# Taking weights apart in one step of 1024 columns per engine, for those whose two low halves VectorE makes

## The chip, the cores and the metric

The kernel runs on one core of one Trainium2 chip. The core has five engines that each work through a queue of their own in order: TensorE (PE, matrix products; PEld are its weight loads), VectorE (DVE), ScalarE (ACT), GpSimd (POOL) and SyncE (SP), which here only issues DMAs. They wait for each other by semaphores. The metric is the device time of one execution in microseconds (us).

## What is computed

One layer of a hybrid model over 512 latent tokens and 256 context tokens, all in float32. The last part, in which most of this case plays, is a mixture of 16384 single-neuron experts:

```
px = split_in(modulate(x) @ w_in)            # projections of the tokens, 10240 columns
mix = merge(gates, hgrn(..), conv(..), att(..)) @ w_out
x = LN(alpha*x + gate*mix)
t = modulate(x)
s1, s2 = scores of 128 keys each, 8 heads    # q = t @ wq
expert, g = top 16 of the summed scores, softmax
act = gelu(u_tab[expert] . t)                # per token, head and k
peer = sum of g * act * v_tab[expert]
x = LN(alpha*x + gate2*peer)
```

The kernel computes the experts of 384 of the 512 tokens densely: all 128 blocks of 128 experts, `a = gelu(uT[i] . t)`, times a gate that is zero where an expert was not chosen, then `acc += a . v[i]`. The first 128 tokens are done by gathering the rows that they chose (256 rows per partition, from u and then from v).

## The kernel before

**Weights in two parts.** A float32 product is made of three faster ones: each operand x is taken apart into a rounded part `hi` and the rest `lo = x - hi`, and `mm3` (lines 140 to 144) adds lo.hi, hi.lo and hi.hi. A weight block is 128 partitions by 1024 columns (512 KB). `wload` (line 120) fetches one into a buffer `wraw` (three of these, SP issues the DMA on line 124 as soon as one is free), and takes it apart in two halves of 512 columns: ScalarE copies a half to `whi` (line 129), VectorE or GpSimd subtracts it into `wlo` (line 131). The argument `subs` names the engines of the two subtractions: (V, V) for 328 blocks, (V, G) or (G, G) for 80. `whi` and `wlo` have eight buffers of 512 columns each, so four blocks.

**Order.** PE, DVE, ACT and POOL run their instructions in the order in which the code is written. Only SP's DMAs are placed by a scheduler.

**Stages.** 590 to 790 us: the output products of the recurrence and the convolution; for each of eight j a merge-gate block (V, V) and a convolution block (V, G) are loaded. 790 to 1100: attention. 1200 to 1380: choice of the experts. 1380 to 1640: the first half of the dense products `uT`, beside the making of gates. From 1640 on the loop over the 128 expert blocks (the loop `for i in range(NT - LAST)` in the code).

**The loop.** Iteration i prepares block n = i + 1 and then multiplies block i. `weigh` makes VectorE multiply the activations by the gates (line 1601), and takes the product apart: ScalarE copies `ph` (line 137), VectorE subtracts `pl` (line 138). Then `wload` of v[n] follows: ScalarE copies `whi`, VectorE subtracts `wlo`. TensorE runs 18 products of 512 columns (`second`). Between them VectorE takes in one or two gathered rows (line 1488 for u, later 1496 for v, each 128x1024), which GpSimd fetches (line 1477). Up to iteration 69 (1640 to 1937 us) the activations were made before. From iteration 70 on (1937 to 2380 us) each iteration also loads u[n+1], right after `weigh`, runs 24 products of 384 columns (`first`) and takes in three or four rows; eight of these iterations have one VectorE step more (lines 1678 and 1681). Every eight iterations five DMAs fetch the next gates (`gr`, line 1589).

Of the kernel before, what the change touches and what calls it, by code (L numbers as in the profile page):

```python
# [9 lines left out]
F32 = mybir.dt.float32  # L10
F32R = mybir.dt.float32r
# [6 lines left out]
AF = mybir.ActivationFunctionType  # L18
# [4 lines left out]
T, TC, D, KT = 512, 256, 1024, 8  # L23
# [71 lines left out]
def body(tc, I, O):  # L95
    nc = tc.nc
    V, A, P, G = nc.vector, nc.scalar, nc.tensor, nc.gpsimd
# [8 lines left out]
    es = ExitStack()  # L106
    const = es.enter_context(tc.tile_pool(name="const", bufs=1))
    wes = ExitStack()
    wp = es.enter_context(tc.tile_pool(name="w", bufs=8))
    pms_ = ExitStack()  # L110
    pmm = pms_.enter_context(tc.tile_pool(name="pmm", bufs=3, space=PSUM))

# [7 lines left out]
    def wload(src, subs=(V, V), raw=None):  # L120

        raw = wp.tile([128, KT, 128], F32, name="wraw", bufs=3) if raw is None else raw
        if src is not None:
            nc.sync.dma_start(raw, src)
        his, los = [], []
        for i in range(2):
            r = raw[:, 4 * i:4 * i + 4, :]
            hi = wp.tile([128, 4, 128], F32R, name="whi")
            A.activation(hi, r, AF.Copy)  # L129
            lo = wp.tile([128, 4, 128], F32R, name="wlo")  # L130
            subs[i].tensor_sub(lo, r, hi.bitcast(F32))  # L131
            his.append(hi)
            los.append(lo)
        return his, los

    def split(hi, lo, src):
        A.activation(hi, src, AF.Copy)  # L137
# [124 lines left out]
    def fetch_next(n=3):  # L262

        if todo and len(ready) < n:
            w = todo.pop(0)
            src, subs = source(*w)
            if w[0] == 'ada':
                raw = wp.tile([128, KT, 128], F32, name="wraw", bufs=3)
                nc.sync.dma_start(raw, src)
                ready.append((w, raw))  # L270
                return
            ready.append((w, wload(None, subs, loaded.pop(0)) if loaded else wload(src, subs)))

    def feed(*w):
        fetch_next(1)
        tag, t_ = ready.pop(0)
        assert tag == w, (tag, w)
        return t_
# [35 lines left out]
    def ada_weights(q_):  # L314
        fetch_raw(7)
        return wload(None, (V, V) if not queue and not raws[1:] else (V, G), raws.pop(0))
# [711 lines left out]
    for g in range(4):  # L1028
        n = 8 * g
        if g == 3:  # L1030
            slot(n, (qb,), (qb,))
            m_ = chain([mgate(j) for j in range(KT)])
            for h in range(2):
                for i, nm in ((0, "kh"), (1, "kl")) if h == 0 else ((0, "vh"), (1, "vl")):
                    t_ = ap_.tile([128, T + TC] if h == 0 else [128, NS, 128], F32R, name=nm)
# [48 lines left out]
    for j in range(KT):  # L1084
        if j % 2 == 0:
            wout(j // 2)
        w = feed('att', j)
# [139 lines left out]
    parts1(0, tfs)  # L1227
    UV = {}
    UV['q', 0] = wload(I['wq'][0], (V, G))
    fetch_next(4)  # L1230
    turn_back(tfs)
# [216 lines left out]
    for b in range(1, NB):  # L1448
# [4 lines left out]
        sl = slice((b - 1) * 128, b * 128)  # L1453
# [341 lines left out]
```

## Time and profile before

| what | value |
|---|---|
| three runs, us | 2467.76 median, 2458.68 to 2470.45 |
| the profiled execution: its own time | 2469.7 |
| its span, first to last instruction | 2467.8 |
| mean granted TensorE clock (share of 2.4 GHz) | 0.986 |
| PE busy | 2356.6 us, 95% |
| DVE busy | 1937.8 us, 79% |
| ACT busy | 1044.3 us, 42% |
| POOL busy | 667.5 us, 27% |
| `wlo` on DVE, wraw blocks (680 of 512 columns) | 453.1 us busy, 186.1 us idle before them |
| `whi` on ACT, wraw blocks (784 of 512 columns) | 447.5 us busy |

The span is that of one profiled execution; 1.9 us of its own time lie around it. Busy shares are means over stages with different limits, and a busy PE is one with a matmul in flight, since matmuls overlap.

### The profile page before, as it was taken

What the parts mean: (1) busy time and instruction counts of PE and PEld (TensorE: products, weight loads), DVE (VectorE), ACT (ScalarE), POOL (GpSimd) and SP (SyncE); (2) the same over time, 40 slices, a digit from 0 to 9 for tenths busy, and PEclk for the clock granted to TensorE, in tenths of its full rate; (3) what the DMA queues carried; (4) which work ended last, traced back from release to release, by engine and by line L of the source; (5) the groups of instructions that cost most, each with busy time, mean ns of one, the idle gap of its engine ahead of it and who ended that gap; (6) DMA issues with size and microseconds to landing.
All of it is one profiled execution on the core that took longest, in us unless ns stands there. A gap on an engine that the chain in (4) does not pass through costs nothing.

```text
span 2467.8 us, 34756 instructions
## 1 busy us (share of the span) xinstructions
PE 2356.6 (95%) x12547; PEld 2028.7 (82%) x12547; DVE 1937.8 (79%) x3722; ACT 1044.3 (42%) x2298; POOL 667.5 (27%) x564
## 2 busy tenths in 40 slices
PE   7999999999988999999999999999999999999997
PEld 3888888887767777787899999987777889898886
DVE  7788888887665566564899789968878888889886
ACT  5544444434312444643457655533333333333333
POOL 6000000003122000031688401122323344444432
PEclk9999999999999999999999999999999999999999
DMA  6211111112364111132333368999999989999962
GB/s 243 69 60 61 61 60 60 52 65 72 134 212 158 43 35 35 52 111 103 105 112 103 121 241 308 330 321 317 335 368 348 350 317 344 324 336 320 331 223 96
DMA packets 156973, 452.66 MB, mean 183 GB/s; under 512 B 16256, under 2 KB 60672, under 8 KB 154624
## 3 DMA queue, kind: packets, MB, share of 16 engines
q1 hardware_dynamic: 106976, 278.33, 32.7%
q0 software_dynamic: 36864, 134.23, 15.3%
q10 hardware_dynamic: 12960, 37.87, 4.1%
q8 instruction: 99, 1.62, 0.3%
q14 instruction: 74, 0.61, 0.1%
HBM read 411.77 MB, written 37.03 MB: 182 GB/s over the span
## 4 chain that ended last, share of the span: by engine, by line
PE 57%; DVE 25%; DMA 6%; ACT 5%; issue 4%; POOL 2%; ACTq 0%; DVEq 0%; SPq 0%; POOLq 0%
PE mm L142 13%; PE mm L144 12%; PE mm L143 12%; DVE wlo L131 6%; DVE raw L1488 3%; DVE ttok L1496 3%; DMA wraw<-in_v_dram 3%; ACT whi L129 2%; PE sc L466 2%; PE pg L1538 2%; ACT ph L137 2%; DMA wraw<-in_uT_dram 2%; PE acc L142 1%; PE acc L143 1%; PE acc L144 1%
## 5 line engine op out<-in xcount | busy, mean ns | idle before, releaser
L131 DVE TENSOR_TENSOR wlo<-wraw,whi 128x512 fp32r<-128x512 f32 x680 | 453.1, 708 | 186.1 <-ACT whi L129 184.2
L142 PE MATMUL mm<-xh,wlo 128*128 128x512 f32 (+1 forms) x1456 | 559.7, 384 | 17.8 <-DVE wlo L131 5.5
L143 PE MATMUL mm<-xl,whi 128*128 128x512 f32 (+1 forms) x1456 | 540.3, 371 | 1.1 <-POOL xl L327 0.9
L144 PE MATMUL mm<-xh,whi 128*128 128x512 f32 (+1 forms) x1456 | 540.5, 371 | 0.0
L129 ACT ACTIVATE whi<-wraw 128x512 fp32r<-128x512 f32 x784 | 447.5, 621 | 121.3 <-DMA wraw<-in_w_in_dram 46.2
L142 PE MATMUL acc<-whi,pl 128*128 128x512 f32 x756 | 300.4, 397 | 23.9 <-DVE pl L138 18.8
L142 PEld LDWEIGHTS mm<-xh,wlo 128*128 128x128 f32 x1456 | 275.8, 189 | 53.1 <-DVE wlo L131 6.8
L144 PEld LDWEIGHTS mm<-xh,whi 128*128 128x128 f32 x1456 | 275.0, 189 | 37.2
L143 PEld LDWEIGHTS mm<-xl,whi 128*128 128x128 f32 x1456 | 275.8, 189 | 34.0 <-DVE xl L327 1.8
L143 PE MATMUL acc<-wlo,ph 128*128 128x512 f32 x756 | 301.5, 399 | 2.1 <-DVE wlo L131 0.9
L144 PE MATMUL acc<-whi,ph 128*128 128x512 f32 x756 | 298.6, 395 | 0.0
L1477 POOL DMA_INDIRECT raw<-in_u_dram,idx x128 | 147.4, 1151 | 472.1 <-DVE act L1488 413.5
L1477 POOL DMA_INDIRECT raw<-in_v_dram,idx x128 | 160.5, 1254 | 193.0 <-DVE ttok L1496 156.1
L142 PEld LDWEIGHTS acc<-whi,pl 128*128 128x128 f32 x756 | 143.8, 190 | 62.4 <-ACT whi L129 16.7
L137 ACT ACTIVATE ph<-a 128x384 fp32r<-128x384 f32 x94 | 49.4, 525 | 332.5 <-DVE a L1601 323.3
L561 DVE SCALAR_TENSOR_TENSOR u<-up,dw,u 128x512 f32<-128x512 f32 x240 | 179.6, 748 | 4.9
L131 POOL TENSOR_TENSOR wlo<-wraw,whi 128x512 fp32r<-128x512 f32 x104 | 149.2, 1457 | 123.0 <-ACT whi L129 116.6
L143 PEld LDWEIGHTS acc<-wlo,ph 128*128 128x128 f32 x756 | 143.7, 190 | 42.7 <-DVE wlo L131 13.4
L144 PEld LDWEIGHTS acc<-whi,ph 128*128 128x128 f32 x756 | 143.6, 190 | 28.5
L1496 DVE SCALAR_TENSOR_TENSOR ttok<-raw,act,ttok 128x1024 f32<-128x1024 f32 x127 | 162.9, 1283 | 3.1
L142 PE MATMUL pa<-xh,wlo 128*128 128x384 f32 x456 | 154.7, 339 | 6.4 <-DVE wlo L131 6.4
L144 PE MATMUL pa<-xh,whi 128*128 128x384 f32 x456 | 154.5, 339 | 0.0
(422 smaller groups left out, 4255.6 us busy)
## 6 DMA issues: line engine op xcount, KB each, us to landing
wraw<-in_uT_dram SPq DMA_DIRECT2D x128, 512.0 KB, 5.0
wraw<-in_v_dram SPq DMA_DIRECT2D x128, 512.0 KB, 6.2
wraw<-in_w_in_dram SPq DMA_DIRECT2D x96, 512.0 KB, 3.3
gd<-gs ACTq DMA_DIRECT2D x16, 1536.0 KB, 7.5
gr<-gd SPq DMA_DIRECT2D x60, 288.0 KB, 9.1
wraw<-in_w_adaT_dram SPq DMA_DIRECT2D x32, 512.0 KB, 4.4
wraw<-in_wq_dram SPq DMA_DIRECT2D x16, 512.0 KB, 3.3
ad<-a ACTq DMA_DIRECT2D x39, 192.0 KB, 4.2
```

The lines of the kernel that those rows point to most:

```text
L129: A.activation(hi, r, AF.Copy)
L131: subs[i].tensor_sub(lo, r, hi.bitcast(F32))
L137: A.activation(hi, src, AF.Copy)
L142: P.matmul(out, ll, rh, start=first, stop=False)
L143: P.matmul(out, lh, rl, start=False, stop=False)
L144: P.matmul(out, lh, rh, start=False, stop=last)
L466: P.matmul(x_.ps[:, b, :], x_.KM[:, b * 128:(b + 1) * 128], ap3(x_.QP, T + b * 128, [2 * w_, 64 // w_], [w_ - T, 2], [1, w_]), start=True, ...
L561: V.scalar_tensor_tensor(acc, up[:, i:i + T], dw[:, j, i:i + 1], acc, op0=ALU.mult, op1=ALU.add)
L1477: G.indirect_dma_start(out=r, out_offset=None, in_=I['u'] if n < NS_ else I['v'], in_offset=bass.IndirectOffsetOnAxis(ap=idx0[:, n % NS_:n ...
L1488: V.tensor_tensor_reduce(out=r, in0=r, in1=ttok, scale=1.0, scalar=0.0, op0=ALU.mult, op1=ALU.add, accum_out=act[:, s_:s_ + 1])
L1496: V.scalar_tensor_tensor(ysb, r, act[:, s_:s_ + 1], ysb, op0=ALU.mult, op1=ALU.add)
L1538: P.matmul(ps[:, i, :], o3[:, q_, :, i], o1[:, i, :], start=q_ == 0, stop=q_ == 1)
```

## The change

For (V, V) blocks ScalarE now copies all 1024 columns in one instruction and VectorE subtracts all 1024 in one. For the other blocks the two halves stay. `whi` and `wlo` become four buffers of 1024 columns, of the same size in all, and each comes free as a whole.

```
-    wp = es.enter_context(tc.tile_pool(name="w", bufs=8))
+    wp = es.enter_context(tc.tile_pool(name="w", bufs=4))
...
-        his, los = [], []
-        for i in range(2):
-            r = raw[:, 4 * i:4 * i + 4, :]
-            hi = wp.tile([128, 4, 128], F32R, name="whi")
-            A.activation(hi, r, AF.Copy)
-            lo = wp.tile([128, 4, 128], F32R, name="wlo")
-            subs[i].tensor_sub(lo, r, hi.bitcast(F32))
-            his.append(hi)
-            los.append(lo)
-        return his, los
+        halves = [slice(0, 4), slice(4, 8)]
+        hi = wp.tile([128, KT, 128], F32R, name="whi")
+        lo = wp.tile([128, KT, 128], F32R, name="wlo")
+        for sl, eng in ([(slice(0, 8), V)] if subs == (V, V) else zip(halves, subs)):
+            A.activation(hi[:, sl, :], raw[:, sl, :], AF.Copy)
+            eng.tensor_sub(lo[:, sl, :], raw[:, sl, :], hi[:, sl, :].bitcast(F32))
+        return [[t_[:, sl, :] for sl in halves] for t_ in (hi, lo)]
```

VectorE in the loop before 1937 us, one iteration before the change (gt and gr are activations and gates, ISA is the step that takes in a row):

```order
L1601 TENSOR_TENSOR gt<-gt,gr 128x384
L138 TENSOR_TENSOR pl<-gt,ph 128x384
L131 TENSOR_TENSOR wlo<-wraw,whi 128x512 x2
L1488 ISA raw,act<-raw,ttok 128x1024
L1488 ISA act 128x1
```

The same iteration after it (lines behind the edit are three lower):

```order
L1598 TENSOR_TENSOR gt<-gt,gr 128x384
L135 TENSOR_TENSOR pl<-gt,ph 128x384
L130 TENSOR_TENSOR wlo<-wraw,whi 128x1024
L1485 ISA raw,act<-raw,ttok 128x1024
L1485 ISA act 128x1
```

Two subtractions have become one, at the same place. ScalarE in the same iterations, before:

```order
L137 ACTIVATE ph<-gt 128x384
L129 ACTIVATE whi<-wraw 128x512 x2
L137 ACTIVATE ph<-gt 128x384
L129 ACTIVATE whi<-wraw 128x512 x2
L137 ACTIVATE ph<-gt 128x384
```

and after:

```order
L134 ACTIVATE ph<-gt 128x384
L129 ACTIVATE whi<-wraw 128x1024
L134 ACTIVATE ph<-gt 128x384
L129 ACTIVATE whi<-wraw 128x1024
L134 ACTIVATE ph<-gt 128x384
```

The copy stays behind `ph` of the same iteration, now as one instruction. Whatever waits for it waits for all 1024 columns. PE and POOL have the same instructions in the same order as before. SP's DMAs in the loop, before (`gr` are the gates, `wraw` the blocks of v):

```order
L124 DMA wraw<-in_v_dram 128x1024 x7
L1589 DMA gr<-gd 128x3x192 x3
L124 DMA wraw<-in_v_dram 128x1024
L1589 DMA gr<-gd 128x3x192
L1589 DMA gr<-gd 128x4x192
```

and after:

```order
L124 DMA wraw<-in_v_dram 128x1024 x7
L1586 DMA gr<-gd 128x3x192 x4
L124 DMA wraw<-in_v_dram 128x1024
L1586 DMA gr<-gd 128x4x192
L124 DMA wraw<-in_v_dram 128x1024 x7
```

One gate DMA more stands ahead of one v block, in four rounds of eight iterations; up to iteration 70 a few more DMAs trade places, and from there on SP's order is the same in both.

## Rows read from the trace of the kernel before

**Rows 1.** Stretches (span us, busy us and instructions, clock, DMA share, GB/s)
```profile
590.00:790.00 200.00, 177.59 (x751) 140.81 (x750) 122.95 (x183) 55.44 (x98) 50.90 (x29) 0.95 0.48 163
...
1640.00:1937.00 297.00, 284.30 (x1198) 221.47 (x1197) 241.24 (x423) 104.20 (x198) 86.20 (x79) 0.99 0.96 343
1937.00:2380.00 443.00, 426.70 (x2112) 383.99 (x2111) 382.46 (x505) 156.47 (x304) 197.39 (x156) 0.98 0.92 327
```

**Rows 2.** Chain that ended last, 1692 to 1712 (start, us, what)
```profile
1699.82 0.53 ACT ph L137
1700.35 0.53 ACT whi L129
...
1700.90 1.29 DVE wlo L131 x2
```

**Rows 3.** VectorE in order of time, 1694 to 1700 (start, us, instruction, idle before)
```profile
1695.05 0.55 DVE L1601 TENSOR_TENSOR gt<-gt,gr 128x384 f32<-128x384 f32 x1
1696.28 0.56 DVE L138 TENSOR_TENSOR pl<-gt,ph 128x384 fp32r<-128x384 f32 x1 [0.67 <-ACT ph L137]
1696.80 1.30 DVE L131 TENSOR_TENSOR wlo<-wraw,whi 128x512 fp32r<-128x512 f32 x2
1698.01 1.22 DVE L1488 CUSTOM_DVE_ANT_0 raw<-raw,ttok 128x1024 f32<-128x1024 f32 x1
...
1699.15 0.55 DVE L1601 TENSOR_TENSOR gt<-gt,gr 128x384 f32<-128x384 f32 x1
```

**Rows 4.** ScalarE in order of time, the same stretch
```profile
1696.15 1.14 ACT L129 ACTIVATE whi<-wraw 128x512 fp32r<-128x512 f32 x2
```

**Rows 5.** ScalarE groups by shape, whole span
```profile
L1072 ACT ACTIVATE xh<-wraw 128x1024 fp32r<-128x1024 f32 x4 | 4.2, 1048 | 1.9 <-DMA wraw<-in_w_out_dram 1.9
```

**Rows 6.** VectorE in order of time, 2218 to 2224
```profile
2220.74 1.22 DVE L1678 TENSOR_TENSOR gt<-gt 128x1024 f32<-128x1024 f32 x1
2221.88 1.29 DVE L131 TENSOR_TENSOR wlo<-wraw,whi 128x512 fp32r<-128x512 f32 x2
```

**Rows 7.** VectorE groups by shape, 1640 to 1937
```profile
L131 DVE TENSOR_TENSOR wlo<-wraw,whi 128x512 fp32r<-128x512 f32 x132 | 85.3, 688 | 8.9 <-ACT whi L129 8.9
```

**Rows 8.** VectorE groups by shape, 1937 to 2380
```profile
L131 DVE TENSOR_TENSOR wlo<-wraw,whi 128x512 fp32r<-128x512 f32 x202 | 130.2, 686 | 23.8 <-ACT whi L129 23.8
...
L1678 DVE TENSOR_TENSOR gt<-gt 128x1024 f32<-128x1024 f32 x4 | 4.9, 1217 | 0.0
L1681 DVE TENSOR_TENSOR gt<-gt 128x1024 f32<-128x1024 f32 x4 | 4.9, 1217 | 0.0
```

**Rows 9.** VectorE in order of time, 2155 to 2166
```profile
2157.28 0.56 DVE L138 TENSOR_TENSOR pl<-a,ph 128x384 fp32r<-128x384 f32 x1 [0.65 <-ACT ph L137]
2157.81 1.29 DVE L131 TENSOR_TENSOR wlo<-wraw,whi 128x512 fp32r<-128x512 f32 x2
```

**Rows 10.** Matmuls in order of time, 1699.5 to 1703
```profile
1699.49 0.39 PE L142 MATMUL acc<-whi,pl 128*128 128x512 f32 x1
...
1701.53 0.39 PE L142 MATMUL acc<-whi,pl 128*128 128x512 f32 x1
```

**Rows 11.** TensorE's weight loads' waits, 1640 to 1937 (total us, times, longest)
```profile
PEld acc L142 <- ACT whi L129: 16.7, 15, 2.1
PEld acc L143 <- DVE wlo L131: 13.2, 45, 0.5
```

**Rows 12.** Chain that ended last, 720 to 756
```profile
735.16 3.53 DMA wraw<-in_w_in_dram
738.77 0.64 ACT whi L129
739.43 0.70 DVE wlo L131
740.17 0.50 PE mm L142
```

**Rows 13.** VectorE's waits, 790 to 1100
```profile
DVE wlo L131 <- ACT whi L129: 27.3, 13, 4.3
```

## Prediction

> **What bounds the kernel now.** I read the table of stretches first. TensorE is busy nearly all the time everywhere, but the two long loop stretches (1640 to 1937 and 1937 to 2380 us) leave it 13 and 16 us short, and the merge-gate stretch (590 to 790 us) 22 us [rows 1]. A busy PE only says that a matmul was in flight, so next I asked for the chain of work that ended last. In the first loop stretch there is no matmul in it: it goes round from ScalarE's `ph` to its `whi`, to VectorE's `wlo` and on through VectorE to the next `ph` [rows 2]. VectorE in order of time says the same. Its cycle runs from one gate product to the next, 1695.05 to 1699.15, so 4.10 us; it has a single gap, 0.67 us, in which it waits for `ph`, and ScalarE can make `ph` only from the gate product that VectorE has just finished [rows 3]. TensorE needs about as long: nine matmuls take 1701.53 - 1699.49 = 2.04 us, so the 18 of an iteration 4.08 [rows 10]. A second row taken in makes VectorE's cycle longer by what one row holds it, 1698.01 to 1699.15, 1.14 us [rows 3], and TensorE's not at all; accordingly it is TensorE that waits for the weights, 45 times for `wlo` and 15 times for `whi` [rows 11]. So a wait that is added to VectorE's cycle there is added to the time, for TensorE has no more than 0.02 us of need beyond the cycle, and nothing else on VectorE's path can run meanwhile.
>
> **What the change does to one iteration.** Now ScalarE starts the two `whi` copies at 1696.15 [rows 4], and VectorE starts on `wlo` at 1696.80 [rows 3]. The chain shows how the two hang together: the first copy ends at 1700.35 + 0.53 = 1700.88, and the subtraction of that half begins 0.02 us later, while the second half is still being copied [rows 2]. That overlap is what goes. A copy of 1024 columns from a `wraw` buffer is in the trace: 1048 ns [rows 5]. Begun at 1696.15, behind the same `ph`, it ends at 1697.20, and with 0.02 us for the signal VectorE starts at 1697.22, so 0.42 us later. What VectorE gets back: the two halves hold it from 1696.80 to the next start at 1698.01, 1.21 us [rows 3]; a float32 product of 1024 columns holds it from 2220.74 to 2221.88, 1.14 us [rows 6]. That is 0.07 us. Net +0.35 us per iteration. Behind the waiting subtraction stand the taking in of a row and the next gate product, so `ph`, `whi` and TensorE's next weights all come that much later.
>
> The Trainium skill, Perfetto Trace Analysis, section Optimizing Scalar/DVE Operations, puts the fixed cost of a VectorE instruction on SBUF at about 60 ns and says that grouping pays if the engine is saturated; the 0.07 us above agrees. By that rule alone each block would be about 0.06 us cheaper and the kernel faster (the third rival). The same section ends by saying that breaking up instructions lets work complete sooner where they cause bubbles on other engines, which is this cycle's case.
>
> **The sum, by stretches.**
> 1. 1640 to 1937 us: 132 halves, so 66 blocks [rows 7], each in the cycle above: 66 x 0.35 = +23.1 us. Blocks whose DMA lands late cost the same, since VectorE then waits for the copy anyhow.
> 2. 1937 to 2380 us: 202 halves, 101 blocks [rows 8]. Fifty are u blocks, loaded right behind `pl`; there VectorE goes from `pl` to `wlo` without a gap, as it does in the first stretch [rows 3, 9], so these too get +0.35. In eight of them a step of 1024 columns stands between, 4 + 4 in number and 1.22 us long [rows 8], which covers the copy: -0.07. The 51 v blocks are subtracted after three or four rows have been taken in, long after their copy: -0.07. Sum 42 x 0.35 - 59 x 0.07 = 14.7 - 4.1 = +10.6. VectorE's cycle is the path here also: its 382 us busy and its waits of 24 us for late copies [rows 1, 8] and about 0.65 us for each of 50 `ph` [rows 9] make 439 of 443 us.
> 3. 590 to 790 us: eight merge-gate blocks come one after another out of a loop that runs over a DMA. The block lands, `whi` starts at 738.77, `wlo` at 739.43, and TensorE's first product at 740.17, as soon as the first half is subtracted [rows 12]. With whole blocks the copy ends at 739.82, the subtraction of 1.22 us (the 1024 columns of [rows 6]) at 741.06, and TensorE starts 0.9 us later than now. If TensorE came late by itself, only the raw buffer's later return would count, 0.35. I take 0.8, near the upper end, as the row shows TensorE waiting: 8 x 0.8 = +6.4.
> 4. 790 to 1100 us: 13 waits of VectorE for `whi` [rows 13], each longer by 0.35, half of them on the path by my choice: +2.3, between 0 and 4.6.
> 5. Elsewhere TensorE sets the pace with its weights fetched two or three blocks ahead: 0, at most +4.
> 6. Paid back: VectorE waits 8.9 and 23.8 us for copies in the two loop stretches [rows 7, 8], almost all of it for blocks of v and u still on their way, with the DMA engines 96% and 92% busy [rows 1]. With a longer iteration a block has more time to land, about 0.9 us in the first stretch (its buffer is asked for two and a half iterations ahead), 0.4 in the second, and the engines less to carry per us. Bounds: nothing and all of it, -33. I take -9. Against this, SP sends one gate DMA of 288 KB more ahead of a block in four rounds; at 343 GB/s [rows 1] that is 0.84 us each, 0 to +3.4, taken as 0 since a block has some slack in most rounds.
>
> The buffers that come free as a whole cost nothing that I can see: a block takes the place of the one four earlier, and in the loop ScalarE's copy stands behind `ph`, which has to wait for products that come after that block's. Should this cover fail, the copy waits half a block's products, up to 2.04 us [rows 10]. Blocks with GpSimd keep their halves: 0.
>
> Sum 23.1 + 10.6 + 6.4 + 2.3 - 9 = +33.4 us against the profiled execution's own 2469.7, so 2503.1. That execution is 1.9 us above the median of the three runs; against the median, 2467.8, the forecast is 2501 us.
>
> **Rivals.**
> - *The DMA waits give it all back.* The 32.7 us of waits vanish as the loop slows: 23.1 + 10.6 + 6.4 - 32.7 = +7.4, so 2475 us. For it: DMA engines nearly full. Against it: a burst of five gate DMAs lands on top of the blocks every eight iterations whatever the pace, and one iteration's 0.3 us more can't take up waits of several us each. Chance 0.08.
> - *TensorE's clock falls.* The merge-gate stretch, with TensorE 11% idle, was granted a clock of 0.95, the loop 0.99 and 0.98 [rows 1]. With 23 us more idle time the first loop stretch would be at (12.7 + 23.1) / 320 = 11% as well. There it costs nothing, since VectorE's cycle is by then the longer; in the second, 4% on 427 us of matmuls would be +17: 2518 us, or a little more with no payback. Chance 0.08.
> - *Faster: fewer instructions, and the wait isn't there.* If VectorE found the copy ready, it would save 0.07 us on each of 66 + 101 blocks, -11.7, and the time would be 2456 us. This is decided at one point: the whole copy must end before `pl` does, at 1696.84, so it would have to start 0.39 us sooner than 1696.15; but ScalarE is at `ph` until then [rows 2, 4], and its order is fixed. Chance 0.04.
>
> **How the numbers follow.** The forecast has a chance of 0.8. Its own range: with all of the payback that seems likely (-20) and 3 us less elsewhere 2487; with no payback and the upper ends of terms 4 to 6 2520. To hold 8 in 10 with the case of full payback half in it, I give 2482 to 2520. A measurement of this kernel can tell about 0.5% from no change, so "same" is 2455 to 2480: it holds the rival of full payback, and a sliver of the forecast: 0.08. Faster than that is a good half of the third rival, 0.03. Slower: 0.89.
>
> **What the next profile would show.** In the first loop stretch VectorE's cycle at 4.45 us instead of 4.10, with a new gap of about 0.4 us ahead of each `wlo` ended by `whi`, one `whi` of 1.05 us and one `wlo` of 1.22 us; TensorE's waits for `wlo` up by some 20 us; the stretch longer by about 20 us. In the second the gap only ahead of the u blocks. In the merge-gate stretch TensorE's start on a block 2.3 us after `whi` starts. I am wrong if that gap is missing, if the cycle stays at 4.10 with the gap there (then something I took for the path had slack), or if the waits for late blocks shrink by as much as the gaps add.

## The result, and the profile after

The changed kernel takes 2494.86 us (median, 2493.89 to 2500.97), the one before 2463.73 us in runs beside it: a ratio of 1.0129, interval 1.0101 to 1.0158. It is slower by 31 us; the forecast was 2501. The profiled execution took 2500.97 us, 31.3 more than that of before; both lie some 6 us above their medians. Line numbers behind the edit are 3 lower now (`ph` and `pl` L134 and L135, the gate product L1598); `whi` stays L129 and `wlo` is L130.

The stretches after, in the columns of [rows 1]:
```profile
590.00:790.00 200.00, 174.19 (x737) 137.77 (x736) 122.63 (x167) 54.28 (x86) 46.80 (x30) 0.96 0.49 161
1640.00:1937.00 297.00, 276.88 (x1119) 206.09 (x1118) 222.86 (x334) 91.62 (x125) 80.41 (x73) 0.99 0.92 321
1937.00:2380.00 443.00, 423.69 (x2079) 375.06 (x2078) 371.49 (x411) 145.86 (x202) 211.45 (x155) 0.99 0.92 329
```
The clock is no lower than it was. Inside the same 297 us VectorE is 18 us and TensorE 7 us less busy than in [rows 1], and TensorE gets through 1119 matmuls instead of 1198. Both engines lost time, so something holds them up in turn. VectorE and ScalarE in order of time, 1701 to 1707 us (start, us, instruction, idle time before it and what ended it), answer to [rows 3, 4]:
```profile
1701.93 0.55 DVE L1598 TENSOR_TENSOR gt<-gt,gr 128x384 f32<-128x384 f32 x1
...
1703.03 1.04 ACT L129 ACTIVATE whi<-wraw 128x1024 fp32r<-128x1024 f32 x1
1703.16 0.56 DVE L135 TENSOR_TENSOR pl<-gt,ph 128x384 fp32r<-128x384 f32 x1 [0.67 <-ACT ph L134]
1704.11 1.23 DVE L130 TENSOR_TENSOR wlo<-wraw,whi 128x1024 fp32r<-128x1024 f32 x1 [0.39 <-ACT whi L129]
1705.25 1.22 DVE L1485 CUSTOM_DVE_ANT_0 raw<-raw,ttok 128x1024 f32<-128x1024 f32 x1
...
1706.39 0.55 DVE L1598 TENSOR_TENSOR gt<-gt,gr 128x384 f32<-128x384 f32 x1
```
The cycle is 1706.39 - 1701.93 = 4.46 us (4.10 before). The 0.67 us for `ph` is as it was; new is 0.39 us for `whi` ahead of `wlo`. The copy starts 0.13 us before `pl` as before, but `wlo` now has to wait for 1.04 us of it instead of 0.53. The single subtraction holds VectorE from 1704.11 to 1705.25, 1.14 us, as the sum had it.

VectorE's group for `wlo`, first the first loop stretch, then the second [rows 7, 8], and last the waits of TensorE's weight loads in the first [rows 11]:
```profile
L130 DVE TENSOR_TENSOR wlo<-wraw,whi 128x1024 fp32r<-128x1024 f32 x62 | 76.0, 1225 | 35.0 <-ACT whi L129 35.0
```
```profile
L130 DVE TENSOR_TENSOR wlo<-wraw,whi 128x1024 fp32r<-128x1024 f32 x100 | 122.2, 1222 | 33.9 <-ACT whi L129 30.8 <-PE pa L141 2.3 <-PE pa L139 0.8
```
```profile
PEld acc L140 <- DVE wlo L130: 38.2, 59, 1.1
PEld acc L139 <- ACT whi L129: 11.0, 14, 1.8
```
In the first stretch VectorE's idle time ahead of `wlo` goes from 8.9 to 35.0 us, and TensorE's wait for `wlo` from 13.2 to 38.2. In the second VectorE's goes only from 23.8 to 33.9.

Both traces hold the same 12,547 matmuls in the same order, so the delay can be read matmul by matmul. By stretches of the kernel before, the changed one loses: 100 to 590 +1.3; 590 to 790 +3.6; 790 to 1100 +0.6; 1100 to 1380 -0.3; 1380 to 1640 +1.3; 1640 to 1937 +21.4; 1937 to 2380 +0.6; from there to the end +2.9; 31.4 in all.

In the merge-gate stretch a block looks like this (ScalarE, VectorE and TensorE, 698 to 703 us; compare [rows 12]):
```profile
698.89 1.06 ACT L129 ACTIVATE whi<-wraw 128x1024 fp32r<-128x1024 f32 x1 [5.75 <-DMA wraw<-in_w_in_dram]
699.99 1.23 DVE L130 TENSOR_TENSOR wlo<-wraw,whi 128x1024 fp32r<-128x1024 f32 x1 [3.05 <-ACT whi L129]
701.26 0.50 PE L139 MATMUL mm<-xh,wlo 128*128 128x512 f32 x1 [2.00 <-DVE wlo L130]
702.10 0.63 PE L139 MATMUL mm<-xh,wlo 128*128 128x512 f32 x1
```
From the copy's start to TensorE's start it is 701.26 - 698.89 = 2.37 us (1.40 in [rows 12]; 2.3 was forecast). The last row shows a second price: 0.84 us after the wait of 2.00 us matmuls hold TensorE 0.63 us instead of 0.39. The granted clock from 702 to 705 us is 0.51 of 2.4 GHz, the 1.2 GHz level.

### The profile page after: what moved, and what is told of

It reads as the page before. It is cut to its first block, busy times and chain, and to the rows that moved or that the text cites. A ratio compares the mean times of both kernels' runs of the same rounds, so it can differ in the third digit from the quotient of the medians.

```text
span 2499.2 us, 33937 instructions
## 1 busy us (share of the span) xinstructions
PE 2364.8 (95%) x12547; PEld 2021.9 (81%) x12547; DVE 1917.3 (77%) x3394; ACT 1012.3 (41%) x1970; POOL 687.3 (28%) x564
## 4 chain that ended last, share of the span: by engine, by line
PE 31%; DVE 24%; ACT 7%; DMA 6%; issue 4%; POOL 1%; ACTq 0%; SPq 0%; POOLq 0%; DVEq 0%
PE mm L139 6%; PE mm L141 6%; PE mm L140 6%; DVE wlo L130 6%; DVE raw L1485 4%; ACT whi L129 4%; DVE ttok L1493 3%; DMA wraw<-in_v_dram 2%; DMA wraw<-in_uT_dram 2%; PE pg L1535 2%; ACT ph L134 2%; DVE eb L1339 1%; PE pa L139 1%; DVE a L1598 1%; PE pa L141 1%
## 5 line engine op out<-in xcount | busy, mean ns | idle before, releaser
L130 DVE TENSOR_TENSOR wlo<-wraw,whi 128x1024 fp32r<-128x1024 f32 (+1 forms) x353 | 428.4, 1217 | 247.9 <-ACT whi L129 230.6
L129 ACT ACTIVATE whi<-wraw 128x1024 fp32r<-128x1024 f32 (+1 forms) x457 | 417.3, 929 | 107.0 <-DMA wraw<-in_w_in_dram 39.7
L140 PE MATMUL acc<-wlo,ph 128*128 128x512 f32 x756 | 304.2, 402 | 16.5 <-DVE wlo L130 11.5
L1474 POOL DMA_INDIRECT raw<-in_u_dram,idx x128 | 152.5, 1192 | 490.8 <-DVE act L1485 431.4
L1474 POOL DMA_INDIRECT raw<-in_v_dram,idx x128 | 174.4, 1362 | 178.5 <-DVE ttok L1493 141.4
L134 ACT ACTIVATE ph<-a 128x384 fp32r<-128x384 f32 x94 | 49.4, 525 | 395.2 <-DVE a L1598 377.0
L130 POOL TENSOR_TENSOR wlo<-wraw,whi 128x512 fp32r<-128x512 f32 x104 | 147.1, 1436 | 130.3 <-ACT whi L129 126.2
```

The source lines that it names most:

```text
L129: A.activation(hi[:, sl, :], raw[:, sl, :], AF.Copy)
L130: eng.tensor_sub(lo[:, sl, :], raw[:, sl, :], hi[:, sl, :].bitcast(F32))
L140: P.matmul(out, lh, rl, start=False, stop=False)
L1474: G.indirect_dma_start(out=r, out_offset=None, in_=I['u'] if n < NS_ else I['v'], in_offset=bass.IndirectOffsetOnAxis(ap=idx0[:, n % NS_:n ...
```

## The experiments

The theory: the price is VectorE's wait for the end of a 1024-column copy, paid where VectorE comes to `wlo` right behind `pl` (or right behind a landing block) and its cycle sets the pace. The rivals: the four buffers, the mere length of either instruction, or a pace set elsewhere. Times are medians; each is set against the kernel before in runs beside it (2464.0 to 2466.1 us).

**Four whole buffers, but halves in both engines.**
```diff
-        for sl, eng in ([(slice(0, 8), V)] if subs == (V, V) else zip(halves, subs)):
+        for sl, eng in zip(halves, subs):
```


> The changed kernel with its four whole buffers, but every block is again copied in two steps of 512 columns by ScalarE and subtracted in two steps of 512 by VectorE. Theory (the price is VectorE's wait for a copy of 1024 columns): the time of the kernel before, 2464 us within 8, and in the first loop's stretch VectorE's cycle is back at 4.10 us from 4.46. Rival (a block's buffers now come free only as a whole, so transfers or copies start later): about the changed kernel's 2495, and the cycle stays near 4.46.


Measured: 2460.66 us, ratio 0.9983 (0.9967 to 0.9999). In the first loop stretch VectorE's group for `wlo` is that of [rows 7] again:
```profile
L130 DVE TENSOR_TENSOR wlo<-wraw,whi 128x512 fp32r<-128x512 f32 x135 | 87.4, 688 | 6.2 <-ACT whi L129 6.2
```
The median cycle of iterations 3 to 65 is 4.16 us again, as before the change (4.51 in the changed kernel). So the buffers are not the loss, and that rival is out. SP's DMAs, however, stand here in the order of the kernel before and not of the changed one, so this run alone does not tell the whole steps from the new order. The trace of the changed kernel does: there the copy starts 0.13 us ahead of `pl` as before, so its block has landed, and the new gap lies behind the copy's start. The whole steps are the loss. The buffers alone gain some 4.7 us (0.2 to 8 by the interval), which neither theory expected. By the matmuls the stretch from 590 to 790 is 5.5 us shorter. The clock there differs (665 to 785 us, columns as in [rows 1]), first before, then this kernel:
```profile
665.00:785.00 120.00, 100.70 (x410) 78.79 (x409) 70.81 (x102) 25.07 (x46) 32.55 (x16) 0.93 0.62 208
```
```profile
665.00:785.00 120.00, 101.32 (x433) 78.67 (x432) 74.13 (x107) 25.55 (x47) 29.19 (x16) 0.97 0.65 211
```
More on this in the last section.

**VectorE in one step, ScalarE in two.**
```diff
-        for sl, eng in ([(slice(0, 8), V)] if subs == (V, V) else zip(halves, subs)):
+        for sl, eng in zip(halves, subs):
             A.activation(hi[:, sl, :], raw[:, sl, :], AF.Copy)
-            eng.tensor_sub(lo[:, sl, :], raw[:, sl, :], hi[:, sl, :].bitcast(F32))
+            if subs != (V, V):
+                eng.tensor_sub(lo[:, sl, :], raw[:, sl, :], hi[:, sl, :].bitcast(F32))
+        if subs == (V, V):
+            V.tensor_sub(lo, raw, hi.bitcast(F32))
```


> The changed kernel with ScalarE's copy in two steps of 512, VectorE's subtraction still in one of 1024. Theory (what counts is when the whole of `whi` is there): the second half's copy ends 1.16 us after the first one's start, against 1.05 for the one copy, so VectorE starts about 0.1 later than in the changed kernel: cycle 4.55 to 4.57 against 4.46, time 2495 + 66 x 0.1 + 42 x 0.1 = about 2505. Rival (the length of ScalarE's single copy is itself the harm, for example because the product's copy `ph` queues behind it): ScalarE's copies are as before, so the time goes back to about 2465.


Measured: 2510.16 us, ratio 1.0176 (1.0155 to 1.0197). In order of time, 1708 to 1714 us:
```profile
1708.76 0.55 DVE L1601 TENSOR_TENSOR gt<-gt,gr 128x384 f32<-128x384 f32 x1
...
1709.86 1.14 ACT L129 ACTIVATE whi<-wraw 128x512 fp32r<-128x512 f32 x2
1709.98 0.56 DVE L138 TENSOR_TENSOR pl<-gt,ph 128x384 fp32r<-128x384 f32 x1 [0.67 <-ACT ph L137]
1711.02 1.23 DVE L133 TENSOR_TENSOR wlo<-wraw,whi 128x1024 fp32r<-128x1024 f32 x1 [0.48 <-ACT whi L129]
...
1713.31 0.56 DVE L1601 TENSOR_TENSOR gt<-gt,gr 128x384 f32<-128x384 f32 x1
```
The two copies end at 1711.00, 0.09 later than one would, the gap is 0.48 and the cycle 4.55. What counts is when the last column of `whi` is there, and the length of ScalarE's instruction is not itself the harm. Against the changed kernel the first loop stretch costs 4 us more and the stretches up to 1100 us 6, where a copy's end counts as well; of the two loops the first was expected to cost 7, and the second, for which 4 were expected, costs nothing.

**ScalarE in one step, VectorE in two.**
```diff
-        for sl, eng in ([(slice(0, 8), V)] if subs == (V, V) else zip(halves, subs)):
-            A.activation(hi[:, sl, :], raw[:, sl, :], AF.Copy)
+        if subs == (V, V):
+            A.activation(hi, raw, AF.Copy)
+        for sl, eng in zip(halves, subs):
+            if subs != (V, V):
+                A.activation(hi[:, sl, :], raw[:, sl, :], AF.Copy)
             eng.tensor_sub(lo[:, sl, :], raw[:, sl, :], hi[:, sl, :].bitcast(F32))
```


> ScalarE's copy in one step of 1024 columns, VectorE's subtraction in two of 512, four whole buffers. Theory (VectorE waits for the end of the whole copy): the gap of 0.39 us ahead of `wlo` stays and the 0.07 us that one subtraction saves is gone, so the cycle is 4.53 us and the time 2495 + 66 x 0.07 + 42 x 0.07 = about 2502. Rival (VectorE's instruction of 1024 columns is the harm): back near 2465.


Measured: 2500.76 us, ratio 1.0147 (1.0117 to 1.0177). VectorE in order of time, 1707 to 1713 us:
```profile
1707.88 0.55 DVE L1601 TENSOR_TENSOR gt<-gt,gr 128x384 f32<-128x384 f32 x1
...
1710.06 1.29 DVE L133 TENSOR_TENSOR wlo<-wraw,whi 128x512 fp32r<-128x512 f32 x2 [0.39 <-ACT whi L129]
...
1712.41 0.56 DVE L1601 TENSOR_TENSOR gt<-gt,gr 128x384 f32<-128x384 f32 x1
```
With VectorE's old two instructions the gap is there all the same, and the cycle is 1712.41 - 1707.88 = 4.53 us, as expected: gap 0.39, saving of 0.07 gone. VectorE's long instruction is not the harm.

**The `v` block fetched ahead of the weighing, in the first loop.**
```diff
+            if ('v', n) not in UV:
+                fetch(('v', n))
```


> The changed kernel, but in the first loop (iterations up to 69) the `v` block is fetched and taken apart ahead of the gathered rows' weighing instead of behind it; nothing is computed otherwise. Theory (the price is the wait for a copy that starts too late): ScalarE's copy now has other work of VectorE beside it or the wait moves; if the copy is done by the time VectorE comes to `wlo`, its cycle is 4.10 - 0.07 = 4.03 us and the time 2495 - 66 x 0.43 = about 2467; if VectorE comes to `wlo` first, the wait grows and the time stays above 2490. Rival (a step of 1024 columns costs VectorE or the DMA more than two of 512, wherever it stands): the cycle stays near 4.46 and the time near 2495 even where no gap stands ahead of `wlo`.


Measured: 2471.75 us, ratio 1.0024 (1.0012 to 1.0036). ScalarE and VectorE, 1847 to 1852 us:
```profile
1847.94 0.55 DVE L1598 TENSOR_TENSOR a<-a,gr 128x384 f32<-128x384 f32 x1
...
1849.09 1.05 ACT L129 ACTIVATE whi<-wraw 128x1024 fp32r<-128x1024 f32 x1
...
1850.83 1.22 DVE L130 TENSOR_TENSOR wlo<-wraw,whi 128x1024 fp32r<-128x1024 f32 x1
...
1851.97 0.55 DVE L1598 TENSOR_TENSOR a<-a,gr 128x384 f32<-128x384 f32 x1
```
`wlo` now comes behind a row's step, 0.69 us after its copy has ended; no gap, and a cycle of 4.03 us, with the same steps of 1024 columns. By the matmuls the stretch is back at the time of before (-0.8 us, against +21.4). It gains nothing beyond that; VectorE's idle time ahead of `wlo` is 19.5 us there, against 8.9 in [rows 7], and ScalarE's copies wait 21.6 us for blocks that land late, against 8.3 before:
```profile
L130 DVE TENSOR_TENSOR wlo<-wraw,whi 128x1024 fp32r<-128x1024 f32 x67 | 81.8, 1222 | 19.5 <-ACT whi L129 14.6 <-issue 4.8
```
The whole step costs nothing where its copy has ended. The time is 5 us above the 2467 expected.

**Whole steps in one place at a time**, all with four whole buffers. First the first loop's `v` blocks alone:
```diff
-        for sl, eng in ([(slice(0, 8), V)] if subs == (V, V) else zip(halves, subs)):
+        for sl, eng in ([(slice(0, 8), V)] if whole else zip(halves, subs)):
...
-        UV[item] = wload(src, SUBS[kind])
+        UV[item] = wload(src, SUBS[kind], whole=kind == 'v' and i < NU)
```


> Whole steps only for the `v` blocks of the first 71 iterations, halves in all other blocks (the two merges, the `u` blocks, the second loop's `v` blocks); four whole buffers. Theory: the first loop's stretch carries 66 x 0.36 = 23.8 less the DMA waits paid back, 21 us in the changed kernel's trace, so the time is 2464 + 21 = 2485, and the stretch from 1640 is as long as in the changed kernel. Rival (the time is lost by the steps elsewhere, the stretch only shows it): under 2475.


Measured: 2474.73 us, ratio 1.0037 (1.0023 to 1.0051). That lies under the bound set for the rival, but the mechanism is the theory's: in the trace the stretch loses 18.3 us, the median cycle is 4.51 us instead of 4.16 (iterations 3 to 65, two-row ones among them), and no other stretch loses more than 0.8. The expectation had started from before; from four buffers with halves, 2460.7, it is +14 by the times (the profiled execution was 5 us slower than the median).

The second loop's `v` blocks alone (`whole=kind == 'v' and i >= NU`):

> Whole steps only for the `v` blocks of the second loop (iterations 71 and later), where rows are weighed between the copy's start and `wlo` and no gap stood ahead of it; halves elsewhere; four whole buffers. Theory: no wait is added there and each such block saves VectorE 0.07 us, at most 51 x 0.07 = 3.6: 2460 us, or 2464 where it is not on the path. Rival (a whole step costs something besides the wait): above 2470.


Measured: 2460.81 us, ratio 0.9982 (0.9968 to 0.9996): no different from halves. VectorE's idle time ahead of the 50 whole ones from 1937 to 2380 us is small:
```profile
L130 DVE TENSOR_TENSOR wlo<-wraw,whi 128x1024 fp32r<-128x1024 f32 x50 | 61.0, 1220 | 2.4 <-ACT whi L129 2.4
```
So the blocks that I had called covered are covered; the 0.07 us that each should save does not show in the time.

All blocks but those of `u` and `v` (`whole=False` where these are loaded, else by `subs == (V, V)`):

> Four whole buffers; whole steps only outside the `u`, `v` blocks of the two loops and of the products behind the merges, that is in the merges and the products up to 1100 us; halves in every `u` and `v` block. Theory (the forecast's terms 3 and 2, now against the kernel with four whole buffers and halves, 2461, whose product that follows each gate's block of `wlo` started 1.2 us after TensorE's last): the changed kernel's trace against that one has +1.6 from 100 to 590, +9.0 from 590 to 790 and +2.0 from 790 to 1100, so the time is 2461 + 12.6 = 2473. Rival (what that trace lost from 590 to 790 is TensorE's granted clock of that one run, not the whole step): 2461 + 4 = 2465.


Measured: 2473.43 us, ratio 1.0035 (1.002 to 1.0049). TensorE's waits for `wlo` from 590 to 800 us, with four buffers and halves, then here:
```profile
PE mm L139 <- DVE wlo L130: 16.5, 9, 2.0
```
```profile
PE mm L139 <- DVE wlo L130: 21.7, 14, 2.1
```
+5.2 us of waits, and the clock from 665 to 785 us is at 0.94, as in the changed kernel, instead of 0.97. By the matmuls 590 to 790 is 6.7 us longer than with halves, and 1.5 and 2.0 us are lost in the stretches around it. The theory's 12.6 is met, 12.0 by the differences to before. An estimate of the clock's share from these two traces: from 640 to 800 us 31 matmuls follow each other at 0.42 us here and 17 with halves; 14 more at 0.19 us each are 2.7 of the 6.7 us, so the longer part is the wait.

The `u` blocks alone (`whole=kind == 'u'`):

> Four whole buffers; whole steps only for the `u` blocks (50 of them in the second loop, the others from 1380 to 1640), halves elsewhere. Theory (VectorE's cycle sets the second loop's pace too): 42 blocks with no rows ahead lose 0.26 each as in the changed kernel's trace, 10.9, and 1.3 from 1380 to 1640: 2461 + 12 = 2473. Rival (the second loop is bound by the DMA, so the wait for the copy takes the place of a wait for the transfer; the changed kernel's trace lost only 0.6 there): 2461 + 2 = 2463.


Measured: 2467.50 us, ratio 1.0008 (0.9998 to 1.0019), between the two. VectorE's groups for `wlo` from 1937 to 2380 us:
```profile
L130 DVE TENSOR_TENSOR wlo<-wraw,whi 128x512 fp32r<-128x512 f32 x98 | 63.1, 685 | 0.7 <-ACT whi L129 0.6
L130 DVE TENSOR_TENSOR wlo<-wraw,whi 128x1024 fp32r<-128x1024 f32 x50 | 61.2, 1224 | 31.6 <-ACT whi L129 31.2 <-PE pa L141 0.4
```
All of the wait stands ahead of the `u` blocks: 42 x 0.39 = 16.4 us is the copy, the other 15 are late transfers, which were 20.3 in the kernel with halves. So a part of the wait for the copy takes the place of one for the transfer: the commonest cycle is 8.37 us instead of 8.01, but the time grows by 6.1 us in place of 12 (against four buffers with halves, each by its difference to before).

Set against four buffers with halves, each by its difference to before in its own runs, the places add up: 14.1 (first loop) + 1.5 (second loop's `v`) + 12.0 (merges) + 6.1 (`u`) - 4.7 (buffers) = +29, where the whole change has +31. Each term is uncertain by some 4 us, as the intervals show.

**The other end of the same rule: fill VectorE's gap.** If VectorE's cycle sets the pace, then taking out its other wait, the 0.67 us for `ph`, must make the kernel before faster. One row's step moves to between `ph` and `pl` (and the second loop keeps one row back for it):
```diff
-        split(ph[i2][0], ph[i2][1], a_)
+        A.activation(ph[i2][0], a_, AF.Copy)
+        if todo:
+            todo.pop(0)()
+        V.tensor_sub(ph[i2][1], a_, ph[i2][0].bitcast(F32))
...
```


> The kernel before, with one gathered row's step moved, in each weighing, from behind the product's subtraction `pl` to between its copy `ph` (ScalarE) and `pl` (VectorE). In the first loop VectorE waits 0.67 us there for `ph`; the moved step has 0.6 to 0.7 us of work. Theory (VectorE's cycle of 4.10 us, waits included, sets the first loop's pace): the cycle falls towards 3.45, until TensorE or the DMA bounds it; TensorE has 276.9 us of work in that stretch of 297, so 10 to 20 us are gained: 2445 to 2455. Rival (the stretch is bound by TensorE or the DMA and VectorE's waits are slack): 2464, and then the changed kernel's loss is not by VectorE's cycle.


Measured: 2431.39 us, ratio 0.9861 (0.983 to 0.9892), more than expected. ScalarE and VectorE in the first loop, then the two loop stretches, then VectorE's group for `pl` in the second, in the kernel before and here:
```profile
1660.95 1.14 ACT L129 ACTIVATE whi<-wraw 128x512 fp32r<-128x512 f32 x2
1661.45 0.56 DVE L1599 TENSOR_TENSOR pl<-gt,ph 128x384 fp32r<-128x384 f32 x1
1661.92 1.29 DVE L131 TENSOR_TENSOR wlo<-wraw,whi 128x512 fp32r<-128x512 f32 x2
```
```profile
1640.00:1937.00 297.00, 290.35 (x1273) 237.66 (x1272) 250.83 (x447) 113.55 (x214) 81.98 (x83) 1.00 0.99 362
1937.00:2380.00 443.00, 437.73 (x2199) 396.52 (x2198) 385.20 (x517) 163.66 (x317) 199.05 (x157) 0.99 0.89 326
```
```profile
L138 DVE TENSOR_TENSOR pl<-a,ph 128x384 fp32r<-128x384 f32 x50 | 28.0, 561 | 33.3 <-ACT ph L137 33.3
```
```profile
L1599 DVE TENSOR_TENSOR pl<-a,ph 128x384 fp32r<-128x384 f32 x53 | 29.2, 551 | 1.9 <-ACT ph L1596 1.9
```
There is no gap ahead of `pl` in this iteration; over the first loop stretch 18.3 us of them are left of 46.8, and 1.9 of 33.3 in the second. Part of that comes back as longer waits ahead of `wlo`: 27.9 us in the first stretch and 53.6 in the second, against 8.9 and 23.8 [rows 7, 8]. By the matmuls the first loop gains 15.7 us, until TensorE is busy for 290 of 297 us and the DMA engines for 99%, and the second gains 21.5. I had put the gain in the first loop alone. VectorE's cycle was the pace in both.

The same in the changed kernel:

> The changed kernel with the same step moved to between `ph` and `pl`. VectorE now comes to `wlo` later against ScalarE's copy only if the copy starts no later; the copy is queued behind `ph`, the moved step lies behind `ph` and ahead of `pl`, so at the end of `pl` the copy has run 0.67 us longer than before and the gap of 0.39 ahead of `wlo` vanishes. Theory: no gap, 0.07 us a block saved: the time of the kernel before with the same step moved, or up to 7 us less. Rival (a whole step costs something besides that wait): 20 to 30 us above it.


Measured: 2439.30 us, ratio 0.9898 (0.9869 to 0.9927), 8 us slower than the run above: neither the theory's 0 to 7 less nor the rival's 20 to 30 more. The two profiled executions are 12 us apart: 8 are lost ahead of the loops, as in the changed kernel, which the expectation had left out; the second loop gives 2 back; and the first loses 5, because the gap does not always vanish:
```profile
1805.81 0.53 ACT L1593 ACTIVATE ph<-a 128x384 fp32r<-128x384 f32 x1 [2.78 <-PE acc L141]
...
1806.24 1.04 ACT L129 ACTIVATE whi<-wraw 128x1024 fp32r<-128x1024 f32 x1
...
1807.31 1.23 DVE L130 TENSOR_TENSOR wlo<-wraw,whi 128x1024 fp32r<-128x1024 f32 x1 [0.39 <-ACT whi L129]
```
VectorE is now ahead of TensorE; `ph`, and the copy queued behind it, wait for TensorE's products, and the copy is again late for `wlo`. Over that stretch VectorE is idle 46.5 us ahead of `wlo`, 27.9 in the run above.

**Both finds together: the filled gap and four whole buffers with halves.**

> The kernel before with both finds together: the gathered row's step between `ph` and `pl` (2431 by itself) and four whole buffers with halves (4.7 us less by themselves). If the two add: 2427. If the four buffers' gain was chance: 2431 or above.


Measured: 2421.19 us, ratio 0.9826 (0.9808 to 0.9843): the best of all, 45 us under before and 74 under the changed kernel, and 6 less than the two finds added. The two loop stretches:
```profile
1640.00:1937.00 297.00, 292.90 (x1292) 242.46 (x1293) 256.97 (x455) 113.50 (x215) 86.23 (x86) 0.99 0.99 360
1937.00:2380.00 443.00, 439.18 (x2220) 399.29 (x2219) 380.35 (x509) 165.98 (x321) 193.99 (x152) 1.00 0.88 322
```
TensorE's shortfall is 4 us in each, 13 and 16 in [rows 1].

With whole steps for the second loop's `v` blocks on top:

> As the run with the row's step and four whole buffers, with whole steps for the second loop's `v` blocks. Theory (no wait is added there, but the copy now ends with the weighed rows ahead moved): between 3.6 us less than that run and the same. Rival (the second loop is then bound by the DMA, a later end of a whole copy shows on TensorE): up to 5 us more.


Measured: 2423.61 us, ratio 0.9828 (0.9812 to 0.9845): no different.

## Why the prediction was right, and where two errors met

- *Bound and mechanism.* Right. The cycle is 4.46 us (4.45 forecast), the gap 0.39, the single subtraction 1.14. The two half-changes and the fetch ahead give cycles of 4.55, 4.53 and 4.03, each what the arithmetic of the copy's end and the subtraction's length says. VectorE is the pace here and yet has 0.67 us of gap in 4.10, and ScalarE, 42% busy over the span, is what it waits for. The Trainium skill, Perfetto Trace Analysis, section Optimizing Scalar/DVE Operations, says that grouping can pay if the engine is saturated, and that breaking up may help where the engine is not saturated but causes bubbles on others; the runs side with the second half.
- *Term 1, first loop, +23.1.* 66 cycles of 0.36 are 23.8; the waits for late blocks shrink by 2.4 (over the same 63 iterations VectorE's idle time ahead of `wlo` is 31.1, of which 63 x 0.39 = 24.6 is the copy, so 6.5 is left of 8.9). 21.4 in the trace; whole steps in this stretch alone cost 18.3 in their trace and 14 by the times.
- *Term 2, second loop, +10.6.* Right for which blocks pay. The commonest cycle grew by 0.26 us (8.01 to 8.27), which holds the `u` block's loss (0.36 by itself) and the `v` block's saving; 42 x 0.26 = 10.9. In the trace of the whole change 0.6 is left against before, and 4.4 against halves in the same buffers. Late transfers take 33.9 - 42 x 0.39 = 17.5 us instead of 23.8 (20.3 with halves in the same buffers), which pays back 6.3 (2.8). In either comparison some 4 us more are gone than that, and why is open. `u` blocks alone cost 6.1 us over the whole kernel.
- *Term 3, merge gates, +6.4.* The price of a block was right (0.97 us against 0.9), and so were the waits: from 590 to 800 us TensorE waits 22.7 us for `wlo`, 16.5 with halves in the same buffers, 6.2 more. The stretch lost 9.1 us against those halves (6.7 with the merges alone). The rest is the clock, which the term lacked: 32 matmuls at 0.42 us instead of 17, an estimated 15 x 0.19 = 2.9.
- *Term 4, +2.3.* 2.0 us against halves in the same buffers, with the merges alone too. Right in size; that half of the waits lie on the path was a choice, and no run tests it.
- *Term 5, elsewhere 0, at most +4.* +1.3 and +1.3, and +2.9 in the tail from 2380 us on (3.2 with the `u` blocks alone, 0.0 with halves): 5, a little over the bound.
- *Term 6, paid back 9.* 2.4 and 6.3: 8.7, right as a choice between bounds 33 us apart, so partly luck. The gate DMAs cost nothing that shows; in the traces seven rounds, not four, send one more ahead of a block (and one is 0.86 us at 343 GB/s, not 0.84).
- *Buffers, 0.* Wrong: -4.7 us by the times, and 5.5 and 1.4 in the traces of 590 to 790 and 790 to 1100. This step failed, and hid behind terms 3 and 5 being too small; that the sum came out 2 us from the trace is partly luck. The traces are single executions: the changed kernel's and that of four buffers with halves lie 40.8 us apart, the times, each against before, 36.
- *Rivals.* The waits did not give everything back (8.7 of 32.7). The clock of the loops did not fall, 0.99 in both stretches. From 665 to 785 us, among the merge gates, it is the one that moves between these kernels: 0.93 before, 0.94 here, 0.97 with four buffers and halves. The copy was ready only where other work stood ahead of `wlo`. (By the times that the third rival names, its copy would have had to start 0.36 us sooner, not 0.39.)

## What to carry to other kernels

Where one engine's result is the other's input, two short steps let the second engine start after half of the first one's work; merging them saves a fixed cost per instruction (0.07 us here) and adds the rest of the producer's time (0.39) wherever the consumer stands waiting, so merge only steps whose input has long been ready. Here even that gained nothing that the times show (2460.81 us against 2460.66, and 2423.61 against 2421.19). Read from the cycle of the engine that sets the pace which gaps are in it: filling the other gap with work that was there anyway (0.67 us for `ph`) gained 33 us, more than the change lost.

## What was not expected of the hardware

Four whole buffers instead of eight halves, with the same instructions, gain 4.7 us, and the gain shows from 590 to 790 us as a higher granted clock. Behind some of TensorE's waits of 2 us, 6 to 8 matmuls follow 0.42 us apart instead of 0.23, the 1.2 GHz level. Between 640 and 800 us there are 37 of these in each of the two traces with eight halves, and 17, 17, 23, 11, 18 and 24 in the six with four whole buffers and halves there; with VectorE's whole steps there it is 31 to 45, and 23 with whole copies but VectorE's halves. The 20 fewer of the first such run are worth an estimated 20 x 0.19 = 3.8 of its 5.5 us. In the six traces the stretch from 590 to 790 is 5.0 to 8.1 us shorter than before, and in the second trace with eight halves 0.2 longer; SP's order up to there is the same in all of them. TensorE waits for `wlo` just as long with eight buffers as with four (16.5 us in 9 waits in both), and the waits ahead of a slow and of a normal product are alike (1.99 us ahead of either, before), so why the clock falls less often is not settled. Another 1.7 us of the gain is a wait for `ms` (2.8 us before, 1.1 with four buffers), also unexplained.
